# When the two attention branches' outputs are split into high and low halves: eleven scheduling ticks behind their loads instead of seven

## The chip, the cores and the metric

The kernel runs on one core of one Trainium2 chip, as one program with one launch. The metric is the device time of an execution in microseconds. The profile is one more execution, taken by the hardware profiler; its times count from the start of its span. The engines are TensorE (PE in the rows, with PEld for its weight loads), VectorE (DVE), ScalarE (ACT), GpSimd (POOL) and SyncE (SP). ACT, POOL and SP also issue DMAs; such an issue stands in the same in-order queue as the engine's other work.

## The reference, cut to what matters

One inference step of one decoder layer, for a prompt of 512 tokens (with 16 learned meta tokens ahead) and for a group of 8 sequences of 8 new tokens each with 2048 cached ones. Two attention branches run on the same normalised input; their outputs go through one output matrix each, are gated and added, and go through w_o:

```python
of = o_fox.reshape(n, l, FOX_WIDTH)
og = (ogn.reshape(n, l, GLA_V) * gla_norm_g.astype(F32) * jax.nn.silu(r.astype(F32))).astype(r.dtype)
branch_f = of @ w_fox_out
branch_g = og @ w_gla_out
merged = jax.nn.sigmoid(gate_f) * branch_f + jax.nn.sigmoid(gate_g) * branch_g
return merged @ w_o
```

Behind this stands a mixture of 32 experts, which the change does not touch. The stretch in question is the last part of the cached attention, which for the 8 sequences reads paged keys and values and computes

```python
s_past = jnp.einsum('nthd,nshd->nhts', q, k_past) * scale + a_q + r.transpose(0, 2, 1)[:, :, None, :]
p = jax.nn.softmax(jnp.concatenate([s_past, s_new], axis=-1), axis=-1).astype(v.dtype)
return jnp.einsum('nhts,nshd->nthd', p[..., :p_len], v_past) + jnp.einsum('nhts,nshd->nthd', p[..., p_len:], v)
```

## The kernel before, in words

Activations that feed large matrix products are kept as two numbers, a high half (hi, what a copy to a rounded 32-bit type leaves) and a low half (lo, the rest), so that three products at the faster rate stand for one exact product: `mm3` (line 138) issues hi*hi, hi*lo and lo*hi for each of the contraction's tiles. A split is two instructions: ACT copies the raw tile to the high half (line 123), and DVE or POOL subtracts (line 125).

Three strands of work are interleaved on TensorE in an order that the program writes out by hand (`manual_schedule` for PE): **dense**, the projections with w_in, of which the output gates are the last; **S**, the cached attention; and the other branch (GLA), which is finished when the stretch in question begins. One turn of the dense strand is half an output tile, 24 matmuls of 288 columns; for a gate ACT then applies a tanh (tile sm, line 1059) and issues the store of the result to DRAM (gtd, line 1060). In S a page of keys (K) or values (V) is one megabyte, gathered by an indirect DMA that POOL issues (line 892) as soon as TensorE has used the page that held one of the three buffers before. DVE transposes each K page (line 1017); TensorE makes scores (line 925); DVE, ACT and again DVE do the softmax (lines 939 to 962: biases R are added, the maximum goes through M, the exponentials are the tile SP, the diagonal block PN, and line 961 scales SP); TensorE transposes SP (line 968), multiplies with the V pages (line 988), ACT copies the result out (SO, line 998), and TensorE turns it round (line 1001).

The prompt's part of both branch outputs has been written to DRAM (ofd and ogd). `branch_inputs` brings it back: eight loads on the SP queue, of 128 rows by 512 (rawf, four) or 576 numbers (rawg, four), and then eight splits, high halves ofh and ogh on ACT, low halves ofl and ogl on POOL, two tiles at a time. The splits are pinned to the place in ACT's and POOL's order at which they are written. `branch_inputs` is a generator; each `yield` is a tick. The outer loop at line 1630 advances it once a turn (line 1631), between two steps of S and ahead of one turn of dense, so a number of ticks is a number of such turns. The splits' results are first needed by the merge (`merge`, from line 1092), which begins when S and dense are at an end; it reads two gate rows at a time from gtd (gt, line 1088). The merge's tiles take the room that rawf and rawg held.

Every DMA of SP or ACT signals its landing on one of eight semaphores (DMAHW0 to DMAHW7 in the order below), handed out in turn over both queues. A DMA that is given a semaphore waits, in its issuer's queue, until the one before it on that semaphore has landed, unless its issuer has already waited for that. Here the four rawf loads have numbers 0, 2, 3 and 4, the four rawg loads 5, 6, 7 and 1. The software DMAs of POOL have eight of their own (DMASW).

## Time and profile before

| what | value |
|---|---|
| device time, median of 3 runs | 975.14 us |
| lowest and highest of them | 973.74 and 982.65 us |
| profiled execution's own time | 978.69 us |
| its span | 976.7 us |
| TensorE busy | 889.1 us, 91% of the span |
| DVE, ACT, POOL busy | 54%, 29%, 29% |
| PE clock granted, mean | 0.959 |

The span is the stretch between the first and the last instruction that the profiler recorded; 2.0 us of the execution lie around it. The profiled execution took 3.55 us more than the median of the runs, which is inside their own spread of 8.91 us. Busy shares are means over stages that have different limits.

### The profile page before, as it was taken

Reading aid. Unit: us, or ns where it says so; the run is one execution under the profiler, and the core shown is the slowest. Engines: PE = TensorE matmul, PEld = TensorE weight load, DVE = VectorE, ACT = ScalarE, POOL = GpSimd, SP = SyncE. Lnnn points to the kernel's source line nnn. Section 1 sums busy time; section 2 is a strip of 40 time slices with the busy share of each in tenths; the row PEclk is TensorE's granted clock in tenths of the full one; section 3 lists DMA queues with packets and bytes.
Section 4 is the critical chain, followed back from the end, with each engine's and each line's share of the span. In section 5 each row is a group of like instructions: output and inputs, shape, how many; then the busy total and the mean of one; then the engine's idle time right before and its main releaser. Section 6 shows DMA issues by size and latency. Waiting matters only on the chain. (4 is left out here: it accounts for less than half of the span.)

```text
span 976.7 us, 18830 instructions
## 1 busy us (share of the span) xinstructions
PE 889.1 (91%) x7680; PEld 680.6 (70%) x7680; DVE 524.5 (54%) x1151; ACT 281.7 (29%) x615; POOL 279.1 (29%) x377
## 2 busy tenths in 40 slices
PE   3989989998799999897989898999499999999995
PEld 3878868788788899796888898999334434443343
DVE  5644545447766667663674256326436545564545
ACT  4114445342334324232233234116111111111113
POOL 5221101124244322241253144212573132211001
PEclk9999989998899999999799999999599999999999
DMA  7252222268369788789898756942679999999922
GB/s 212 66 130 62 90 79 65 60 240 310 117 216 344 285 276 280 224 315 375 287 341 304 253 177 189 310 183 97 225 275 407 410 406 413 409 410 412 385 91 99
DMA packets 124655, 239.98 MB, mean 246 GB/s; under 512 B 15812, under 2 KB 89452, under 8 KB 108180
## 3 DMA queue, kind: packets, MB, share of 16 engines
q1 hardware_dynamic: 107268, 160.78, 47.2%
q0 software_dynamic: 12432, 72.37, 20.0%
q10 hardware_dynamic: 4864, 5.57, 1.7%
q8 instruction: 62, 1.02, 0.4%
q14 instruction: 29, 0.24, 0.1%
HBM read 226.53 MB, written 15.83 MB: 248 GB/s over the span
## 5 line engine op out<-in xcount | busy, mean ns | idle before, releaser
L138 PE MATMUL pj<-hth,wh 128*128 128x288 f32 (+2 forms) x656 | 207.8, 317 | 2.1 <-DVE kt L381 1.8
L138 PE MATMUL pj<-hth,wl 128*128 128x288 f32 (+2 forms) x656 | 200.3, 305 | 0.4 <-DVE wl L125 0.4
L138 PE MATMUL pj<-htl,wh 128*128 128x288 f32 (+2 forms) x656 | 200.1, 305 | 0.0
L138 PEld LDWEIGHTS pj<-hth,wh 128*128 128x128 f32 (+1 forms) x656 | 127.1, 194 | 12.2 <-issue 7.5
L138 PEld LDWEIGHTS pj<-hth,wl 128*128 128x128 f32 (+1 forms) x656 | 126.5, 193 | 1.7 <-DVE wl L125 0.6
L138 PEld LDWEIGHTS pj<-htl,wh 128*128 128x128 f32 (+1 forms) x656 | 127.3, 194 | 0.5
L1353 PE MATMUL pj<-wgu,xt 128*64 128x512 f32 x512 | 117.7, 603 | 9.7 <-DVE xt L1363 9.7
L1326 POOL DMA_INDIRECT xg<-h2d,ix x64 | 65.8, 1028 | 122.9 <-DVE xt L1363 95.7
L1353 PEld LDWEIGHTS pj<-wgu,xt 128*64 128x64 f32 x512 | 36.0, 138 | 75.5 <-issue 65.6
L125 DVE TENSOR_TENSOR wl<-w,wh 128x1024 fp32r<-128x1024 f32 (+1 forms) x41 | 49.8, 1215 | 59.8 <-ACT wh L123 55.5
L1017 DVE STREAM_TRANSPOSE K<-K 128x2048 f32<-128x2048 f32 x32 | 73.5, 2302 | 4.0 <-DMA K<-in_cache_k_dram,idx 3.8
L123 ACT ACTIVATE wh<-w 128x1024 fp32r<-128x1024 f32 (+2 forms) x57 | 52.6, 925 | 59.4 <-PE pj L138 53.0
L1353 PE MATMUL ab<-yh,S 128*128 128x512 f32 (+1 forms) x160 | 66.8, 417 | 1.7 <-DVE x L1418 0.9
L1418 DVE TENSOR_TENSOR x<-x,ab 128x512 f32<-128x512 f32 (+1 forms) x80 | 54.5, 684 | 17.3 <-PE ab L1353 17.3
L1353 PE MATMUL ab<-yl,S 128*128 128x512 f32 (+1 forms) x160 | 63.2, 395 | 0.0
L1353 PE MATMUL dn<-wdn,heT 128*64 128x512 f32 x256 | 58.7, 593 | 1.4 <-ACT heT L1387 1.4
L892 POOL DMA_INDIRECT K<-in_cache_k_dram,idx x32 | 33.9, 1059 | 54.3 <-PE S L925 32.5
L1353 PEld LDWEIGHTS ab<-yh,S 128*128 128x128 f32 (+1 forms) x160 | 28.2, 176 | 27.3 <-DVE x L1418 15.0
L892 POOL DMA_INDIRECT V<-in_cache_v_dram,idx x32 | 32.5, 1016 | 49.0 <-PE tp L988 30.7
L1404 DVE SCALAR_TENSOR_TENSOR yl<-dn,gate,yh 128x512 fp32r<-128x512 f32 x32 | 24.0, 751 | 40.7 <-ACT yh L1403 38.1
L1353 PEld LDWEIGHTS dn<-wdn,heT 128*64 128x64 f32 x256 | 19.2, 137 | 37.8 <-issue 34.1
L1387 ACT ACTIVATE heT<-tp 128x256 f32<-128x256 f32 x16 | 6.1, 384 | 118.9 <-PE tp L1356 116.6
(428 smaller groups left out, 1604.4 us busy)
## 6 DMA issues: line engine op xcount, KB each, us to landing
wdn<-in_w_expert_down_dram SPq DMA_DIRECT2D x32, 1024.0 KB
wgu<-in_w_expert_gate_dram SPq DMA_DIRECT2D x32, 1024.0 KB
wgu<-in_w_expert_up_dram SPq DMA_DIRECT2D x32, 1024.0 KB
w<-in_w_in_dram SPq DMA_DIRECT2D x40, 512.0 KB
gtd<-sm ACTq DMA_DIRECT2D x32, 144.0 KB
gt<-gtd SPq DMA_DIRECT2D x8, 576.0 KB
R<-rdr SPq DMA_DIRECT2D x16, 256.0 KB
w<-in_w_o_dram SPq DMA_DIRECT2D x8, 512.0 KB
```

Of the source, the lines that this page charges most:

```text
L123: keep(nc.scalar.activation(hi, raw, AF.Copy))
L125: keep(e.tensor_tensor(lo, raw, hi.bitcast(F32), op=OP.subtract))
L138: nc.tensor.matmul(ps, lhsT=w[:, kt, :], rhs=r[:, kt, cs], start=(kt == 0 and j == 0), stop=(kt == nk - 1 and j == 2))
L892: nc.gpsimd.indirect_dma_start(t, None, view, bass.IndirectOffsetOnAxis(ap=self.idx[:, which, i:i + 1], axis=0)))
L1017: self.tc.keep_in_program_order(nc.vector.transpose(t, t))
L1326: self.nc.gpsimd.indirect_dma_start(xg[:, b * 256:(b + 1) * 256], None, self.h2d.rearrange("t (q f) -> (t q) f", q=4), bass.IndirectOffset ...
L1353: self.tc.keep_in_program_order(self.nc.tensor.matmul(*a, **kw))
L1387: self.nc.scalar.activation(hT, pt[:, 0:256], AF.Copy)
L1404: nc.vector.scalar_tensor_tensor(yl[:, nh], dn, gate, yh[:, nh].bitcast(F32), op0=OP.mult, op1=OP.subtract)
L1418: self.tc.keep_in_program_order(nc.vector.tensor_tensor(x, x, ps[:w], op=OP.add))
```

## The change

The number of ticks between the issue of the loads and the first split goes from 7 to 11.

```diff
--- before.py
+++ after.py
@@ -1075,7 +1075,7 @@
                 raws.append((raw, n))
                 for m in range(4):
                     nc.sync.dma_start(raw[:, m], src[m, :, 0:n])
-            for _ in range(7):
+            for _ in range(11):
                 yield
             for (raw, n), (h, l) in zip(raws, hl):
                 for m in range(4):
```

TensorE's order is the same, row for row, in both programs. On ACT the first two high halves move from between the setting of a query block (QB) and a gate's tanh to a place some 45 rows later. In these rows a name carries its buffer's number, and what stands in brackets are the semaphores that the instruction waits for. ACT before, at the first two splits:

```order
L901 ACTIVATE QB1_1889<-QT_1884 32x16x8 x3
L123 ACTIVATE ofh_5312<-rawf_5311 128x512 [waits DMAHW0_49,Pool_49]
L123 ACTIVATE ofh_5312<-rawf_5311 128x512 [waits DMAHW2_49]
L1059 ACTIVATE sm_3282<-pj_5325 128x288 [waits DMAHW5_49,PE_49]
L1060 DMA gtd_75<-sm_3282 128x288 [waits Activation_49]
L998 ACTIVATE SO_5391<-tp_5087 128x128 [waits PE_49]
L953 ACTIVATE SP_5277,sl_5276<-R_4821,sb_5274 128x512 [waits DVE_49]
L955 ACTIVATE PN_1890,sl_5276<-sN_5261,sb_5274 128x8 [waits Pool_49]
L953 ACTIVATE SP_5277,sl_5276<-R_4821,sb_5274 128x512
L955 ACTIVATE PN_1890,sl_5276<-sN_5261,sb_5274 128x8
L1059 ACTIVATE sm_3282<-pj_5395 128x288 [waits DMAHW1_49,PE_49]
L1060 DMA gtd_75<-sm_3282 128x288 [waits DMAHW5_49,Activation_49]
```

ACT at the same place now:

```order
L901 ACTIVATE QB1_1889<-QT_1884 32x16x8 x3
L1059 ACTIVATE sm_3282<-pj_5325 128x288 [waits DMAHW5_49,PE_49]
L1060 DMA gtd_75<-sm_3282 128x288 [waits DMAHW0_49,Activation_49]
L998 ACTIVATE SO_5391<-tp_5087 128x128 [waits PE_49]
L953 ACTIVATE SP_5277,sl_5276<-R_4821,sb_5274 128x512 [waits DVE_49]
L955 ACTIVATE PN_1890,sl_5276<-sN_5261,sb_5274 128x8 [waits Pool_49]
L953 ACTIVATE SP_5277,sl_5276<-R_4821,sb_5274 128x512
L955 ACTIVATE PN_1890,sl_5276<-sN_5261,sb_5274 128x8
L1059 ACTIVATE sm_3282<-pj_5395 128x288 [waits DMAHW1_49,PE_49]
L1060 DMA gtd_75<-sm_3282 128x288 [waits DMAHW5_49,Activation_49]
L961 ACTIVATE SP_5277<-SP_5277,srl_5291 128x512 [waits DVE_49]
```

The two ofh are gone from here, and the two gtd issues stay; the first of them has gained a wait for DMAHW0, which the first ofh had done before it, and the second waits for DMAHW5 in both programs.

POOL before, from its first low halves on (K and V are page gathers):

```order
L125 TENSOR_TENSOR ofl_5313<-rawf_5311,ofh_5312 128x512 [waits DMAHW0_49,Activation_49]
L125 TENSOR_TENSOR ofl_5313<-rawf_5311,ofh_5312 128x512 [waits DMAHW2_49,Activation_49]
L892 DMA K_5850<-in_cache_k_dram,idx_383 128x2048 [waits DMASW3_49,DVE_49,PE_49]
L125 TENSOR_TENSOR ofl_5313<-rawf_5311,ofh_5312 128x512 [waits DMAHW3_49,Activation_49]
L928 MEMSET PN_1890 128x256 [waits DVE_49,PE_49,Pool_49]
L125 TENSOR_TENSOR ofl_5313<-rawf_5311,ofh_5312 128x512 [waits DMAHW4_49,Activation_49]
L125 TENSOR_TENSOR ogl_5320<-rawg_5318,ogh_5319 128x576 [waits DMAHW5_49,Activation_49]
L125 TENSOR_TENSOR ogl_5320<-rawg_5318,ogh_5319 128x576 [waits DMAHW6_49,Activation_49]
L892 DMA V_5975<-in_cache_v_dram,idx_383 128x2048 [waits DMASW7_49,DMASW4_49,PE_49]
L125 TENSOR_TENSOR ogl_5320<-rawg_5318,ogh_5319 128x576 [waits DMAHW7_49,Activation_49]
L125 TENSOR_TENSOR ogl_5320<-rawg_5318,ogh_5319 128x576 [waits DMAHW1_49,Activation_49]
L892 DMA V_6047<-in_cache_v_dram,idx_383 128x2048 [waits DMASW1_49,PE_49]
```

POOL now, from the last clearing of PN on:

```order
L928 MEMSET PN_1890 128x256 [waits DVE_49,PE_49,Pool_49]
L892 DMA V_5963<-in_cache_v_dram,idx_383 128x2048 [waits DMASW7_49,DMASW4_49,PE_49]
L892 DMA V_6031<-in_cache_v_dram,idx_383 128x2048 [waits DMASW1_49,PE_49]
L125 TENSOR_TENSOR ofl_5313<-rawf_5311,ofh_5312 128x512 [waits DMAHW0_49,Activation_49]
L125 TENSOR_TENSOR ofl_5313<-rawf_5311,ofh_5312 128x512 [waits DMAHW2_49,Activation_49]
L892 DMA V_6153<-in_cache_v_dram,idx_383 128x2048 [waits DMASW6_49,DMASW2_49,PE_49]
L892 DMA V_6212<-in_cache_v_dram,idx_383 128x2048 [waits DMASW4_49,PE_49]
L125 TENSOR_TENSOR ofl_5313<-rawf_5311,ofh_5312 128x512 [waits DMAHW3_49,Activation_49]
L125 TENSOR_TENSOR ofl_5313<-rawf_5311,ofh_5312 128x512 [waits DMAHW4_49,Activation_49]
L125 TENSOR_TENSOR ogl_5320<-rawg_5318,ogh_5319 128x576 [waits DMAHW5_49,Activation_49]
L125 TENSOR_TENSOR ogl_5320<-rawg_5318,ogh_5319 128x576 [waits DMAHW6_49,Activation_49]
L892 DMA V_6287<-in_cache_v_dram,idx_383 128x2048 [waits DMASW5_49,DMASW0_49,PE_49]
```

Before, three more V gathers follow with no split between them; now two ogl follow. The same five V gathers stand in other places between the low halves: two ahead of all eight, two behind the first pair, and the last behind six.

ACT before, from the gate's tanh ahead of the last sequence's softmax on (SO is the result of the sequence before):

```order
L1059 ACTIVATE sm_3282<-pj_6122 128x288 [waits DMAHW2_49,PE_49]
L953 ACTIVATE SP_6102,sl_6101<-R_5748,sb_6099 128x512 [waits DVE_49]
L955 ACTIVATE PN_1890,sl_6101<-sN_6086,sb_6099 128x8 [waits Pool_49]
L953 ACTIVATE SP_6102,sl_6101<-R_5748,sb_6099 128x512
L955 ACTIVATE PN_1890,sl_6101<-sN_6086,sb_6099 128x8
L1060 DMA gtd_75<-sm_3282 128x288 [waits Activation_49]
L998 ACTIVATE SO_6184<-tp_5950 128x128 [waits PE_49]
L961 ACTIVATE SP_6102<-SP_6102,srl_6116 128x512 [waits DVE_49,Activation_49]
L961 ACTIVATE SP_6102<-SP_6102,srl_6116 128x512 [waits Activation_49]
L1059 ACTIVATE sm_3282<-pj_6188 128x288 [waits DMAHW3_49,PE_49]
L1060 DMA gtd_75<-sm_3282 128x288 [waits Activation_49]
L123 ACTIVATE wh_6215<-w8_5994 128x1024 [waits DMAHW6_49]
```

ACT now, from the same tanh on:

```order
L1059 ACTIVATE sm_3282<-pj_6106 128x288 [waits DMAHW2_49,PE_49]
L953 ACTIVATE SP_6086,sl_6085<-R_5748,sb_6083 128x512 [waits DVE_49]
L955 ACTIVATE PN_1890,sl_6085<-sN_6070,sb_6083 128x8 [waits Pool_49]
L953 ACTIVATE SP_6086,sl_6085<-R_5748,sb_6083 128x512
L955 ACTIVATE PN_1890,sl_6085<-sN_6070,sb_6083 128x8
L1060 DMA gtd_75<-sm_3282 128x288 [waits DMAHW5_49,Activation_49]
L123 ACTIVATE ofh_5312<-rawf_5311 128x512 x2
L961 ACTIVATE SP_6086<-SP_6086,srl_6100 128x512 [waits DVE_49,Activation_49]
L961 ACTIVATE SP_6086<-SP_6086,srl_6100 128x512 [waits Activation_49]
L998 ACTIVATE SO_6171<-tp_5942 128x128 [waits PE_49]
L1059 ACTIVATE sm_3282<-pj_6175 128x288 [waits DMAHW3_49,PE_49]
L1060 DMA gtd_75<-sm_3282 128x288 [waits DMAHW6_49,Activation_49]
```

The first two ofh stand ahead of the scaling of SP, and SO has moved behind that scaling. The next two ofh follow the last row shown, and four ogh come behind the next two gate halves.

On SP the eight loads keep their place. The first two gate-row loads (gt) go from ahead of the second branch weight to behind the third, the second of them waits for the last ogl, and one expert weight (wdn) that stood ahead of the load of x2 stands three branch weights later.

## Rows read from the trace of the kernel before

**Rows 1.** Who TensorE (PE) waited for, 440 to 560 us: us in total, times, longest.

```profile
PE tp L1001 <- ACT SO L998: 6.7, 1, 6.7
...
PE tp L968 <- ACT SP L961: 1.8, 1, 1.8
...
PE pj L138 <- DVE wl L125: 0.4, 1, 0.4
```

**Rows 2.** Timeline of ACT and its DMA issues (ACTq), around the first splits.

```profile
459.06 0.63 ACT L123 ACTIVATE ofh<-rawf 128x512 fp32r<-128x512 f32 x1 [7.89 <-DMA rawf<-ofd]
462.16 0.63 ACT L123 ACTIVATE ofh<-rawf 128x512 fp32r<-128x512 f32 x1 [2.48 <-DMA rawf<-ofd]
...
463.12 0.33 ACTq L1060 DMA_DIRECT2D gtd<-sm  x1
463.49 0.28 ACT L998 ACTIVATE SO<-tp 128x128 f32<-128x128 f32 x1 [0.40 <-ACT sm L1059]
...
466.07 0.33 ACTq L1060 DMA_DIRECT2D gtd<-sm  x1
467.16 1.34 ACT L961 ACTIVATE SP<-SP,srl 128x512 f32<-128x512 f32 x2 [1.12 <-DVE srl L959]
```

**Rows 3.** Timeline of TensorE: three instructions that end a wait or follow ACT.

```profile
463.82 0.48 PE L1001 MATMUL tp<-ident,SO 128*128 128x128 f32 x1 [6.74 <-ACT SO L998]
...
526.44 0.27 PE L1001 MATMUL tp<-ident,SO 128*128 128x128 f32 x1
...
541.86 1.64 PE L988 MATMUL tp<-V,PT 128*32 128x128 f32 x32 [3.18 <-DMA V<-in_cache_v_dram,idx]
```

**Rows 4.** Line 138's matmuls in two stretches: busy (count), PE clock, DMA share, GB/s.

```profile
468.00:474.00 6.00, 5.30 (x22) 0.50 0.97 314
476.10:479.10 3.00, 3.00 (x23) 1.00 0.69 155
```

**Rows 5.** Timeline of POOL: low halves, and the last V page's issue.

```profile
495.27 2.53 POOL L125 TENSOR_TENSOR ofl<-rawf,ofh 128x512 fp32r<-128x512 f32 x2
...
509.65 2.81 POOL L125 TENSOR_TENSOR ogl<-rawg,ogh 128x576 fp32r<-128x576 f32 x2
...
532.99 0.95 POOL L892 DMA_INDIRECT V<-in_cache_v_dram,idx  x1 [7.39 <-PE tp L988]
```

**Rows 6.** One stretch: length; PE, PEld, DVE, ACT, POOL; PE clock; DMA; GB/s.

```profile
530.00:540.00 10.00, 8.14 (x139) 7.07 (x138) 0.92 (x3) 1.88 (x3) 1.63 (x2) 1.00 1.02 408
```

**Rows 7.** Timeline of the SP queue: two groups of issues.

```profile
457.48 1.75 SPq L1077 DMA_DIRECT2D rawg<-ogd  x4
...
518.92 2.57 SPq L1088 DMA_DIRECT2D gt<-gtd  x2
```

**Rows 8.** Who the SP queue's DMA issues waited for, 461 to 467 us.

```profile
SPq L130 <- DMA rawf<-ofd: 2.9, 1, 2.9
SPq L908 <- DMA rawf<-ofd: 1.8, 1, 1.8
```

**Rows 9.** Timeline of DVE: short operations, and the merge's first.

```profile
467.35 0.36 DVE L962 TENSOR_SCALAR PN<-PN,srl 128x8 f32<-128x8 f32 x2
...
494.87 3.10 DVE L962 TENSOR_SCALAR PN<-PN,srl 128x8 f32<-128x8 f32 x2
...
520.16 0.96 DVE L945 TENSOR_TENSOR M<-M,aq 128x2 f32<-128x2 f32 x1
...
555.88 0.42 DVE L1102 SCALAR_TENSOR_TENSOR mt<-gt,pj 128x256 f32<-128x256 f32 x1 [5.81 <-PE pj L138]
```

**Rows 10.** Timeline of ACT around the last sequence's softmax.

```profile
508.72 1.26 ACT L123 ACTIVATE ogh<-rawg 128x576 fp32r<-128x576 f32 x2 [0.40 <-ACT sm L1059]
...
524.41 0.28 ACT L998 ACTIVATE SO<-tp 128x128 f32<-128x128 f32 x1
525.84 1.33 ACT L961 ACTIVATE SP<-SP,srl 128x512 f32<-128x512 f32 x2 [1.15 <-DVE ogc L880]
...
531.50 0.41 ACT L1059 ACTIVATE sm<-pj 128x288 f32<-128x288 f32 x1 [2.56 <-PE pj L138]
```

## The prediction

> **What bounds the kernel now.** The stretch in which the change acts ends when TensorE has done the last step of the cached attention, so I read first who TensorE waited for between 440 and 560 us [rows 1]. The longest wait is 6.7 us for SO, ACT's copy of a finished result; 1.8 us for SP, the scaled softmax, follow, both on ACT. ACT's timeline shows why [rows 2]: the first ofh begins at 459.06, having waited 7.89 us for its load, the second at 462.16, when the second load has landed, and behind them stand a gate's tanh, its store, and SO (463.49). TensorE goes on at 463.82 [rows 3]. [...]
>
> What ends the stretch is another thing: TensorE's last step with a V page begins at 541.86 after 3.18 us of waiting for that page [rows 3], which POOL had issued at 532.99 [rows 5]; the DMA engines were full then, at 408 GB/s [rows 6]. From there TensorE runs on into the merge. So a gain at 460 counts as far as it also brings that page forward.
>
> **Part 1, the first two splits leave the gap.** They free ACT of their own two waits, but not of the loads. The store of the gate that stood behind them (gtd) shares its landing semaphore, DMAHW0, with the first rawf load. Before, ofh had waited for that; now the store must, and ACT's queue with it. The load landed by 459.06. From the store to SO ACT took 463.49 - 463.12 = 0.37 us [rows 2], so SO comes at 459.43 and TensorE goes on 0.33 us later, at 459.76: 4.06 us sooner than 463.82.
>
> Then the same again. Next on ACT is the second store, at 466.07 before [rows 2], which waits for DMAHW5, the first rawg load, in both programs. Before, it was reached late and did not show. Now it is reached near 462, and the scaling of SP (467.16) stands behind it. When that load lands no row says, but both sides are bounded. It had landed by 466.07, since the store then went out. It was issued at 457.48 [rows 7], behind four rawf loads, of which one held up an SP issue for 1.8 us [rows 8]. SP's issues before it had waited for the first two loads, and the second landed at 462.16 [rows 2]; so the third landed no sooner than 462.16 + 1.8 = 464.0. The scaling thus begins between 464.0 + 0.37 = 464.4 and 466.07 + 0.37 = 466.4, against 467.16: 0.7 to 2.8 us sooner. It can also be nothing, since the next K page is now asked for 4 us earlier and shares the DMA engines. I take **-0.8 us**, near the late end, because the fourth rawf load stands ahead of the rawg one and the second landed 3.1 us after the first [rows 2], the third 1.8 or more behind that. Of the 6.7 us gap most is not removed: it comes back as a longer wait for SP.
>
> That a DMA issue holds its queue for another load's landing is seen on SP, which waited 2.9 us with a weight load for rawf, whose data it does not need [rows 8]; no row shows ACT doing so. [...]
>
> **Part 2, the first two low halves leave POOL.** At 495.27 they ran for 2.53 us [rows 5], and a DVE pair that takes 0.36 us took 3.10 us beside them [rows 9]. It delayed a weight's low half, for which TensorE waited 0.4 us [rows 1]: **-0.4 us**. Likewise a tiny DVE operation took 0.96 us at 520.16 beside an ogl pair that now moves away; its 0.8 us come off the last sequence's softmax and pay for part of the next item.
>
> **Part 3, what the splits meet where they now stand.** On ACT the first pair, 2 * 0.63 us [rows 2], runs while DVE sums, so the scaling at 525.84 is not held up by it. But SO, at 524.41 before [rows 10], now follows the scaling: 525.84 + 1.33 = 527.17, less the 0.8 and the 1.2 us of parts 1 and 2, is 525.2; plus 0.33 it meets TensorE at 525.5, where TensorE would have been at 526.44 - 1.2 = 525.2 [rows 3]. I take **+0.2 us**; without the 0.8 it is 1.0.
>
> On POOL the last V page now stands behind two ofl and two ogl. The ogl pair hangs on the tanh that began at 531.50 [rows 10]. That tanh moves by -0.8 - 0.4 + 0.2 = -1.0 us to 530.5; then 0.41 for it, 0.40 until ogh begins, 0.63 for one ogh [rows 10] and 2.81 for the pair [rows 5]: the page is issued at 534.75, **1.8 us later** than at 532.99. If its landing takes as long as before (541.86 - 532.99 = 8.87 us), the stretch ends 1.8 us later. Against that, two gate-row loads of 576 KB (2 * 128 * 576 numbers), issued at 518.92 before [rows 7], now come after this page. They were in front of it on engines that were full: 1.18 MB at 408 GB/s are 2.9 us [rows 6]. The end lies between +1.8 - 2.9 = -1.1 and +1.8; I take the middle, **+0.4 us**. It replaces the gains above and is not added to them, since TensorE waits for the page either way. Two earlier V pages go behind the first ofl pair; their steps come ahead of this page's, and the wait moves rather than grows.
>
> **Part 4, edits that cost nothing.** The last two ogl run beside the last dense turns. The two gate-row loads wait for them, near 544; the merge first uses one at 555.88, where DVE waited for TensorE [rows 9], so 12 us cover some 3 us of transfer; without that cover the merge's first product would wait the 3 us. The expert weight that goes three branch weights later is needed only in the experts' stage. TensorE's order does not change.
>
> **Sum.** Against the profiled execution: 978.69 + 0.4 = 979.1 us, whose span was 976.7. That execution was 3.55 us above the median of the runs, so the forecast for the median is 975.14 + 0.4 = **975.5 us**: no change. About 1% (9.75 us) is what a measurement of this kernel can tell from no change; its own three runs spread over 8.91 us.
>
> **Rivals.** *The whole gap goes*: the stores do not hold ACT, or their loads land early in most executions. TensorE gains 6.7 + 1.8 + 2.4 us, and the last page moves along with the tanh: against the forecast's -0.8 this is 10.1 us better, 965.4. For it speaks that the wait shown is for the splits; against it, that the stores' semaphores are in the program. Chance 0.05. *Part of it goes*: the rawg load lands at the early end (-2.8 against -0.8, so -2.0) and the full clock comes back sooner (up to -2.4): 971.1 to 973.5. Chance 0.12.
>
> *The low halves now collide with the softmax* and the kernel is slower. Two operations of DVE that read SBUF alone were stretched by POOL's subtractions [rows 9]; now an ofl pair of 2.53 us [rows 5] falls on the last sequence's chain of sums, reciprocal and scaling on DVE. It decides from the point where one of them, between the sum and the reciprocal, begins behind the first ofl; then the chain, SO and the last page come 2.5 us later. With the page's old 8.87 us this gives 1.8 + 2.5 = +4.3 us, 979.4, and 980.4 if part 1 gains nothing. For it: the pair starts within a microsecond of that chain. Against it: the adding starts as soon as ACT's sums are there, one ofh (0.63 us) ahead of the first ofl. Chance 0.22.
>
> [...]
>
> **How the numbers follow.** Forecast (974 to 978): 0.58; the whole gap 0.05; part of it 0.12; the collision 0.22; slower by over 1%, with both losses and a merge that waits, 0.03. The range from 971 to 980.5 takes in the bounds -1.1 and +1.8, the partial gain and the collision, and leaves out the first and the last. Faster by over 1%: 0.05; within 1%: 0.92; slower: 0.03.
>
> **What would show it.** TensorE's wait for SO falls to about 2.7 us, and its wait for SP grows from 1.8 to about 5; the store ahead of SO begins near 459, the second near 466. The DVE pair near 495 takes 0.36 us again. SO of the last sequence stands behind the scaling. POOL's last V issue follows an ogl pair directly, near 535, and TensorE still waits for that page. I am wrong if either store goes out before its load has landed, if the SP wait does not grow, or if the last page's step moves by more than 3 us.

## The result, and the profile after

The change makes the kernel slower: 980.29 us is the median of 20 runs, against 975.58 us of 20 runs of the kernel before, a ratio of 1.0059 with a 95% interval of 1.0039 to 1.0078. The same kernel compared once more, on another occasion, gave 1.0035 (0.9999 to 1.0070). The profiled execution took 982.93 us, its span is 981.0. The time lies at the upper edge of the range given (971 to 980.5), but the forecast was no change, 975.5, and the change costs some 0.35 to 0.6%.

Up to the store of ogd (line 683) both programs run alike, so I count from it. In the kernel before it is this row of the SP queue,

```profile
442.20 0.36 SPq L683 DMA_DIRECT2D ogd<-og  x1
```

and the scores of the last sequence, a second mark, begin here on TensorE:

```profile
516.03 1.06 PE L925 MATMUL S<-K,QB 128*32 128x128 f32 x32
```

In the changed kernel the SP queue shows the same store, and the two gate-row loads that have moved behind the third branch weight:

```profile
442.69 0.36 SPq L683 DMA_DIRECT2D ogd<-og  x1
...
544.46 2.52 SPq L1088 DMA_DIRECT2D gt<-gtd  x2
```

Who TensorE waited for, in the changed kernel, 440 to 560 us (us in total, times, longest):

```profile
PE tp L968 <- ACT SP L961: 10.3, 1, 10.3
PE tp L988 <- DMA V<-in_cache_v_dram,idx: 4.0, 1, 4.0
PE tp L1001 <- ACT SO L998: 2.0, 2, 1.6
```

Against [rows 1] the wait for SO has nearly gone (of the 2.0 us only 0.4 are at this place), and the wait for SP has grown from 1.8 to 10.3 us: the two waits were 8.5 us together, and are 10.7 at this place now. The second profile of the changed kernel (change_again below) splits them otherwise, 4.1 and 4.3 us, 8.4 together:

```profile
PE tp L1001 <- ACT SO L998: 5.7, 2, 4.1
...
PE tp L968 <- ACT SP L961: 4.3, 1, 4.3
```

ACT's timeline in the first profile says why the wait for SP grew:

```profile
457.26 0.33 ACTq L1060 DMA_DIRECT2D gtd<-sm  x1
457.63 0.28 ACT L998 ACTIVATE SO<-tp 128x128 f32<-128x128 f32 x1 [4.85 <-PE pj L138]
...
459.93 0.39 ACT L1059 ACTIVATE sm<-pj 128x288 f32<-128x288 f32 x1
468.45 0.33 ACTq L1060 DMA_DIRECT2D gtd<-sm  x1
468.82 1.33 ACT L961 ACTIVATE SP<-SP,srl 128x512 f32<-128x512 f32 x2 [8.51 <-DMA rawg<-ogd]
```

The first store goes out at 457.26 and SO follows it, 6 us sooner than in [rows 2]. The gate's tanh runs at 459.93, and then ACT's queue stands still for 8.1 us until the second store goes out at 468.45. The scaling follows, later than before. The hold is named as the landing of rawg.

POOL's timeline has the K page, which k_waits below shows to be behind the late landing, and the later places of the pairs:

```profile
459.61 0.94 POOL L892 DMA_INDIRECT K<-in_cache_k_dram,idx  x1 [3.76 <-PE S L925]
...
525.25 2.51 POOL L125 TENSOR_TENSOR ofl<-rawf,ofh 128x512 fp32r<-128x512 f32 x2 [6.73 <-ACT ofh L123]
527.91 0.96 POOL L892 DMA_INDIRECT V<-in_cache_v_dram,idx  x1
529.18 0.94 POOL L892 DMA_INDIRECT V<-in_cache_v_dram,idx  x1 [0.30 <-PE tp L1001]
...
536.95 2.80 POOL L125 TENSOR_TENSOR ogl<-rawg,ogh 128x576 fp32r<-128x576 f32 x2 [2.46 <-ACT ogh L123]
539.90 0.96 POOL L892 DMA_INDIRECT V<-in_cache_v_dram,idx  x1 [0.16 <-issue]
```

Since SO was early, the next K page was asked for at 459.61; before, it was asked for at 466.47, after the rawg load had landed. In the second profile the first store was itself held for rawf, until 18.25 us behind the store of ogd (14.57 in the first profile), so that SO and the K page came later there, the page 21.59 us behind that store against 16.92.

Further down, two V pages stand behind the first ofl pair, and the last one, at 539.90, behind the first ogl pair ([rows 5]: 532.99). What the two late pages cost is seen on the DMA engines. From 7 to 13 us behind the scores of the last sequence they were full before, and nearly empty with the change (columns as in [rows 6]; the kernel before first, then the changed one):

```profile
523.03:529.03 6.00, 5.84 (x50) 5.34 (x43) 3.48 (x15) 4.33 (x12) 1.80 (x2) 1.00 1.01 328
524.09:530.09 6.00, 4.12 (x30) 3.67 (x29) 3.97 (x13) 4.17 (x11) 4.38 (x4) 0.97 0.17 27
```

The second profiles of the two kernels show the same, with DMA shares of 1.02 and 0.18. Not all of this is the two pages: the change also takes the two gate-row loads out of this stretch, and one V page, which is issued 0.5 us behind the scores instead of 5.2. low_later_11 below has these changes as well, but not the two late pages, and moves 228 GB/s in the same stretch.

DVE's timeline, a short pair and two small operations of the last softmax:

```profile
495.07 0.36 DVE L962 TENSOR_SCALAR PN<-PN,srl 128x8 f32<-128x8 f32 x2
...
521.22 0.16 DVE L945 TENSOR_TENSOR M<-M,aq 128x2 f32<-128x2 f32 x1
...
525.37 1.21 DVE L880 COPY ogc<-ogb 128x32 f32<-128x32 f32 x1
```

The pair of [rows 9] takes 0.36 us again instead of 3.10, and the operation at line 945 0.16 instead of 0.96. But the copy at line 880 takes 1.21 us; it starts 0.12 us after POOL's ofl pair at 525.25.

TensorE at the last sequence's scores, at the turn of SO, and at the last V page's step:

```profile
517.09 1.06 PE L925 MATMUL S<-K,QB 128*32 128x128 f32 x32
...
528.67 0.33 PE L1001 MATMUL tp<-ident,SO 128*128 128x128 f32 x1 [1.60 <-ACT SO L998]
...
545.83 0.86 PE L988 MATMUL tp<-V,PT 128*32 128x128 f32 x24 [4.01 <-DMA V<-in_cache_v_dram,idx]
```

It waits 1.60 us for SO, which now follows the scaling, and then works at a granted clock of 0.50 for a while. The clock is the third figure from the end in this window (length; PE, PEld, DVE, ACT, POOL busy; PE clock; DMA share; GB/s):

```profile
530.80:533.00 2.20, 2.20 (x11) 2.20 (x11) 2.16 (x2) 0.62 (x2) 2.02 (x2) 0.50 0.94 385
```

The chain that ended last passes through the load of rawg, the copy, the ogl pair and the last page's transfer (start, us, what):

```profile
456.58 11.79 DMA rawg<-ogd
...
525.37 1.22 DVE ogc L880
...
536.95 0.58 POOL ogl L125
...
539.90 5.89 DMA V<-in_cache_v_dram,idx
```

Set out by marks, with the second profile of each kernel beside it (each figure is the difference of two start times):

| stretch, us | before | changed | before, 2nd | changed, 2nd | forecast |
|---|---|---|---|---|---|
| store of ogd to the scaling at the first place | 24.96 | 26.13 | 24.73 | 24.82 | -0.8 |
| store of ogd to the scores of the last sequence | 73.83 | 74.40 | 71.36 | 71.37 | -1.2 |
| scores to the scaling of SP | 9.81 | 10.03 | 10.05 | 10.03 | -0.8 |
| scaling to TensorE's turn of SO | 0.60 | 1.55 | 0.33 | 1.55 | +1.0 |
| turn of SO to the next tanh | 5.06 | 6.70 | 5.17 | 5.13 | 0 |
| that tanh to the last V page's issue | 1.49 | 4.53 | 1.50 | 4.53 | +2.8 |
| issue to TensorE's step with the page | 8.87 | 5.93 | 8.09 | 7.25 | -2.9 to 0 |
| scores to that step, sum of five | 25.83 | 28.74 | 25.14 | 28.49 | |

From the step with the last V page to the end of the span it is 434.8 and 439.4 us before, 435.2 and 434.9 after: nothing is lost there. The loss lies in 3.1 us between the scores and the last step, (28.74 + 28.49 - 25.83 - 25.14) / 2, and in what the first place adds: 0.6 us in the first pair of profiles (74.40 - 73.83), nothing in the second (71.37 and 71.36).

### The profile page after: what moved, and what is told of

It is laid out like the page before. It is cut to its first block, busy times and chain, and to the rows that moved or that the text cites. A ratio compares the mean times of both kernels' runs of the same rounds, so it can differ in the third digit from the quotient of the medians.

```text
span 981.0 us, 18832 instructions
## 1 busy us (share of the span) xinstructions
PE 892.2 (91%) x7680; PEld 684.8 (70%) x7680; DVE 521.8 (53%) x1151; ACT 281.8 (29%) x615; POOL 279.3 (28%) x377
## 3 DMA queue, kind: packets, MB, share of 16 engines
q8 instruction: 62, 1.02, 0.4%
## 4 chain that ended last, share of the span: by engine, by line
PE 70%; DVE 9%; DMA 9%; ACT 5%; issue 3%; POOL 3%; ACTq 0%; POOLq 0%; DVEq 0%; SPq 0%
PE pj L138 25%; PE pj L1353 12%; PE ab L1353 6%; PE dn L1353 6%; PE pj L1140 5%; PE S L925 2%; PE tp L988 2%; DMA V<-in_cache_v_dram,idx 1%; DMA out_dram<-s 1%; DMA rawg<-ogd 1%; PE G L523 1%; DVE K L1017 1%; DMA gtd<-sm 1%; PE tp L736 1%; DMA K<-in_cache_k_dram,idx 1%
```

## The experiments

Eighteen runs follow: fifteen other kernels, one of them twice, and both kernels of the change once more. Theory A puts the loss at the last sequence (A1 in its softmax, A2 in the last V page's place on POOL, L both), theory B at the first place or in how pages happen to land, D in the DMA engines, K in the K page asked for early. All figures of this table are worked out from one profile each as in the table above: the scaling at the first place and the scores of the last sequence are counted from the store of ogd, the rest from those scores; "copy" is the duration of line 880 in the last softmax. An interval stands behind each ratio.

| kernel | first scaling | scores | copy | two V pages | tanh | last V issue | its step | ratio to before |
|---|---|---|---|---|---|---|---|---|
| before | 24.96 | 73.83 | 0.18 | 6.90, 8.62 | 15.47 | 16.96 | 25.83 | |
| before_again | 24.73 | 71.36 | 0.42 | 6.87, 8.56 | 15.55 | 17.05 | 25.14 | |
| the change | 26.13 | 74.40 | 1.21 | 10.82, 12.09 | 18.28 | 22.81 | 28.74 | 1.0059 (1.0039 to 1.0078) |
| change_again | 24.82 | 71.37 | 1.20 | 10.84, 12.10 | 16.71 | 21.24 | 28.49 | 1.0035 (0.9999 to 1.0070) |
| low_later_11 | 24.76 | 71.21 | 0.18 | 6.81, 8.53 | 16.86 | 18.35 | 25.53 | 0.9972 (0.9937 to 1.0008) |
| low_later_again | 26.31 | 73.96 | 0.18 | 6.81, 8.47 | 16.80 | 18.29 | 25.57 | 1.0024 (0.9991 to 1.0057) |
| ticks_12 | 26.23 | 76.35 | 0.18 | 6.81, 8.54 | 15.65 | 20.13 | 26.26 | 1.0076 (1.0037 to 1.0115) |
| ticks_14 | 26.29 | 75.11 | 0.18 | 6.84, 8.55 | 15.68 | 17.17 | 25.54 | 1.0070 (1.0039 to 1.0101) |
| first_low_later_11 | 26.63 | 73.74 | 1.30 | 6.02, 7.27 | 18.37 | 22.90 | 28.90 | 1.0053 (1.0031 to 1.0074) |
| g_low_later_11 | 25.51 | 71.75 | 1.20 | 10.83, 12.10 | 16.69 | 18.18 | 27.44 | 1.0037 (1.0014 to 1.0059) |
| first_pair_12 | 26.20 | 74.50 | 0.18 | 6.81, 8.51 | 15.65 | 21.85 | 27.73 | 1.0016 (0.9984 to 1.0049) |
| two_loads_11 | 16.20 | 71.38 | 1.20 | 11.19, 12.46 | 17.05 | 21.58 | 30.22 | 1.0023 (0.9991 to 1.0055) |
| two_loads_low_later_11 | 19.75 | 65.26 | 1.30 | 6.02, 7.27 | 16.79 | 18.28 | 25.39 | 1.0015 (0.9988 to 1.0041) |
| two_loads_first_pair_12 | 16.17 | 72.08 | 0.18 | 6.79, 8.48 | 15.63 | 21.84 | 28.27 | 1.0016 (0.9989 to 1.0043) |
| quarter_loads_11 | 17.32 | 64.50 | 1.20 | 11.20, 12.46 | 17.05 | 21.58 | 27.81 | 0.9946 (0.9912 to 0.9980) |
| last_pair_11 | 24.21 | 71.34 | 1.40 | 11.54, 12.80 | 17.25 | 18.75 | 28.45 | 1.0039 (1.0008 to 1.0070) |
| last_pair_13 | 23.57 | 70.73 | 0.18 | 6.82, 8.51 | 15.66 | 20.20 | 29.20 | 1.0069 (1.0033 to 1.0105) |
| pairs_11_13 | 23.37 | 72.97 | 1.40 | 11.51, 12.77 | 18.79 | 23.34 | 31.82 | 1.0085 (1.0053 to 1.0117) |
| k_waits | 24.27 | 71.42 | 1.20 | 10.84, 12.11 | 16.69 | 21.22 | 28.60 | 1.0028 (0.9996 to 1.0060) |
| low_later_k_waits | 23.90 | 70.84 | 2.53 | 6.03, 7.28 | 19.08 | 20.58 | 27.48 | 1.0001 (0.9973 to 1.0029) |

**Low halves later: low_later_11 and low_later_again.** The low halves of a pair are written one tick behind its high halves:

```diff
-                    self.split(raw[:, m], h[:, m, 0:n], l[:, m, 0:n], "pool", pin=True)
+                    keep(nc.scalar.activation(h[:, m, 0:n], raw[:, m], AF.Copy))
+                    late.append((raw[:, m], h[:, m, 0:n], l[:, m, 0:n]))
                     if m % 2:
                         yield
+                        for r, x, y in late:
+                            keep(nc.gpsimd.tensor_tensor(y, r, x.bitcast(F32), op=OP.subtract))
+                        late = []
```

> Eleven ticks as in the change, but each pair of low halves on POOL is written one tick behind its high halves, so that no low half stands inside the last sequence's softmax and two V pages pass ahead of the first. ACT's order stays that of the change. Theory A (the time is lost at the last sequence: POOL's low halves stretch a DVE copy from 0.18 to 1.21 us, TensorE waits 1.6 us for SO and its clock falls, and the last V page stands behind a pair of ogl): the copy takes 0.2 us again, TensorE waits about 0.6 us for SO, the last V page is issued when TensorE releases its buffer, about 3 us sooner; 3 to 4.5 us faster than the change, 0.996 to 1.001 of the kernel before. Theory B (the time is lost at the first place, where a store waits 8.5 us for a rawg load, and what follows only carries it): as the change, 1.004 to 1.008.

> The kernel with all low halves one tick behind their high halves, a second time and on this chip. Theory L: 25.4 to 25.6 us from the scores of the last sequence to the step with the last V page, 0.994 to 1.001. Theory B: 1.0035 to 1.006, as the change.

Both profiles give the forecast local figure, 25.5 us from scores to step, 3 us less than the change. DVE's timeline in the first of them shows the copy free, and the ofl pair falling on the pair of line 962 instead, which nothing waits for:

```profile
526.06 0.18 DVE L880 COPY ogc<-ogb 128x32 f32<-128x32 f32 x1
...
526.79 2.81 DVE L962 TENSOR_SCALAR PN<-PN,srl 128x8 f32<-128x8 f32 x2
```

The ratios, 0.9972 and 1.0024, lie on either side of 1, the second of them outside the ranges of both theories; taken together the kernel is as fast as before. That speaks for the last sequence. SO still follows the scaling here, and the tanh still comes 1.3 us later than before (16.86 and 16.80 us behind the scores), but the three V pages are not held up behind low halves. Late pages cost the time, then, more than the late tanh by itself.

**Other tick counts: ticks_12 and ticks_14.** The number 11 becomes 12 or 14.

> Twelve ticks. Neither high nor low halves stand inside the last sequence's softmax, and SO stands ahead of the scaling of SP again, as before the change; four ofl stand ahead of the last V page, the second pair hanging on a later tanh. Theory A: no wait of TensorE for SO and full clock there, 3 us sooner than the change at the tanh ahead of the last V page; that page is still issued some 4 us behind this tanh; 0.999 to 1.002 of the kernel before. If it were the POOL queue alone, with nothing from softmax and clock: as the change, 1.004 to 1.008. Theory B: as the change too.

> Fourteen ticks. All five V pages are issued ahead of every low half, and the softmax is free of splits. Theory A: all that the change lost at the last sequence comes back, the last V page is issued about 6 us sooner than in the change, and TensorE no longer waits 4 us for it; 0.992 to 0.998 of the kernel before, unless the merge then waits for the last low halves, which would show as TensorE's wait for POOL near 550. Theory B: 1.004 to 1.008.

The local figures came (25.5 us for fourteen, as before the change), but both runs are slower, by 0.7%. With later splits the gate-row loads stand ahead of other loads on SP, and the second of them waits there for the last ogl. SP's queue in ticks_12 is held for 13 us, and a branch weight goes out behind it:

```profile
552.72 13.05 SPq L1088 DMA_DIRECT2D gt<-gtd  x2
...
573.63 0.46 SPq L130 DMA_DIRECT2D w<-in_w_gla_out_dram  x1
```

TensorE's waits in the merge of ticks_12 (in the change there is no such row):

```profile
PE pj L138 <- ACT wh L123: 4.3, 1, 4.3
```

The prediction had priced an uncovered merge at 3 us, for its gate rows; what TensorE waits for here is a branch weight's high half, whose load stood behind those rows on SP. The gain at the last sequence is bought with 4.3 us of waiting, and 4.9 in ticks_14. With these waits taken off, 1.0032 and 1.0020 would be left: theory A is not met for fourteen ticks (0.992 to 0.998), and where the rest is from was not tried.

**Two DMAs for eight: two_loads_11.**

```diff
-                for m in range(4):
-                    nc.sync.dma_start(raw[:, m], src[m, :, 0:n])
+                nc.sync.dma_start(raw, src[:, :, 0:n].rearrange("m p n -> p m n"))
```

> Eleven ticks, but the four rawf loads are one DMA and the four rawg loads one, so that they take two of the eight landing semaphores and neither of the next two stores of a gate shares one with them. Theory A and B agree that the second store then goes out at once and that TensorE's wait of 10.3 us for SP shrinks by some 8 us, with the full clock kept or back sooner. Theory A: what is lost at the last sequence stays, so the run is 8 to 10 us faster than the change, 0.995 to 0.998 of the kernel before. Theory B: all that was lost goes, 0.985 to 0.992. If a store's shared semaphore is not what holds ACT, the wait for SP stays at about 10 us and the ratio at 1.004 to 1.008.

ACT's timeline shows the second store going out at once, and the scaling 16.20 us behind the store of ogd, 9.9 and 8.6 us earlier than in the change's two profiles:

```profile
460.58 0.39 ACTq L1060 DMA_DIRECT2D gtd<-sm  x1
461.39 1.34 ACT L961 ACTIVATE SP<-SP,srl 128x512 f32<-128x512 f32 x2 [0.85 <-DVE srl L959]
```

So the shared semaphore is what held ACT. But of those 8.6 to 9.9 us little is left at the scores of the last sequence, 71.38 against 74.40 and 71.37. TensorE now waits for pages instead, among other things 4.7 us for a K page, by way of DVE's transposition of it:

```profile
PE tp L988 <- DMA V<-in_cache_v_dram,idx: 6.7, 1, 6.7
PE S L925 <- DVE K L1017: 4.7, 1, 4.7
```

The DMA engines are full all the while (one stretch, columns as in [rows 6]):

```profile
460.00:500.00 40.00, 31.61 (x466) 28.78 (x464) 22.60 (x48) 10.01 (x23) 8.31 (x10) 0.89 1.03 376
```

The forecast of 8 to 10 us was wrong by the same mistake that "the whole gap goes" would have made: the gap at 460 is not free to be won. The gap was 10 us wide, yet pages set the pace behind it.

**Change_again, and one half of the cure each: first_low_later_11 and g_low_later_11.** Here the wait of one tick ahead of the low halves is kept for the first pair alone, or for the two rawg pairs alone:

```diff
                     if m % 2:
-                        yield
+                        if n == 512 and m == 1:
+                            yield
                         for r, x, y in late:
```

with n != 512 as the condition in g_low_later_11; the other pairs have their tick behind the low halves.

> The changed kernel itself, a second profile and a second comparison, as the measure for the three beside it. Ratio to the kernel before 1.004 to 1.008. Counted from the store of ogd by line 683, TensorE's step with the last V page began at 99.7 us before and at 103.1 with the change; if the loss is of this stretch, it begins at 101.5 or later again, and a DVE copy (line 880) of the last softmax takes 1.2 us again.

> As the change, but the first pair of ofl is written one tick later, so that POOL does not subtract beside the last softmax; the last V page still stands behind the first ogl pair. Theory A1 (the loss is in the softmax, from the copy that POOL stretches by 1.0 us and the half clock after TensorE's gap, up to 1.6 us): 1 to 2.6 us faster than the change on this chip, the last V page still issued 4.5 us behind the tanh that precedes it. Theory A2 (the loss is the page's place behind the ogl pair): as the change, within 0.5 us.

> As the change, but the ogl pairs are written one tick later, so that the last V page passes ahead of all four; the ofl pair beside the softmax stays. Theory A2: the page is issued 1.5 us behind the tanh that precedes it instead of 4.5, and the run is 3 us faster than the change. Theory A1: the page is issued sooner, but takes longer to land, since the DMA engines are full, and its step moves by less than 1 us; as the change, with the copy of line 880 at 1.2 us.

In change_again the copy took 1.20 us as expected, and the ratio of 1.0035 lies just below the range given. The step with the last V page missed its bound: it came 99.86 us behind the store of ogd, not at 101.5 or later. That bound had been taken from single profiles; the second profile of the kernel before has 96.50, so that the two pairs of profiles differ by 3.5 and 3.4 us at this step.

first_low_later_11 did not do what it was made for: both V pages went out sooner than ACT's high halves were ready, and POOL's pair still began beside the softmax. Its DVE timeline:

```profile
526.65 1.30 DVE L880 COPY ogc<-ogb 128x32 f32<-128x32 f32 x1
```

It tells only that two V pages issued 5 us earlier bring nothing while the last one stays late. In g_low_later_11 the last V page was free; POOL's timeline shows the two other pages still late, behind the ofl pair,

```profile
520.77 0.96 POOL L892 DMA_INDIRECT V<-in_cache_v_dram,idx  x1 [0.16 <-issue]
522.04 0.95 POOL L892 DMA_INDIRECT V<-in_cache_v_dram,idx  x1 [0.30 <-PE tp L1001]
...
528.12 0.95 POOL L892 DMA_INDIRECT V<-in_cache_v_dram,idx  x1 [0.69 <-PE tp L988]
```

and TensorE's step with the last page came 9.3 us after its issue:

```profile
537.38 0.87 PE L988 MATMUL tp<-V,PT 128*32 128x128 f32 x12 [4.30 <-DMA V<-in_cache_v_dram,idx]
```

27.44 us after the scores is 1.2 less than the mean of the change's two profiles, not 3: A2 alone is refuted. Against the 25.5 us of low_later_11, where the tanh and the last V page came at the same times (16.86 and 18.35 us; here 16.69 and 18.18), it is 1.9 more, and up to that page the two kernels differ at the last sequence in the ofl pairs' places alone, and by them in the two late pages. As with the change, the DMA engines stood nearly empty from 7 to 13 us behind the scores, at 26 GB/s; low_later_11 moved 228. Behind that gap three pages follow one another (405 GB/s from 16 to 19 us), and the last of them lands late though it was issued in time. So the two losses overlap and do not add up: by single profiles the two late pages alone cost 1.9 us here, the last page issued at 22.90 us alone costs 3.4 in first_low_later_11 (28.90 against 25.5), and the change has both for 3.1.

**The two together: two_loads_low_later_11.** Both diffs above.

> One DMA for rawf and one for rawg, and all low halves one tick later than in the change. With four loads each, low halves a tick later gave 0.9972 of the kernel before, and two loads alone gave 1.0023. If both gains hold side by side (the second store no longer waits for rawg, the softmax and the last page are free of POOL): 0.990 to 0.996. If the DMA engines, full in this stretch, set when the pages land whatever ACT does: as low halves later alone, 0.995 to 1.000.

1.0015, above both ranges given: neither gain shows beside the kernel before. The profiled execution was the shortest of its twelve, at 966.34 us, so its early scores (65.26) are not typical.

**Out of the softmax: first_pair_12, and with two loads two_loads_first_pair_12.** The first two pairs are split together at the twelfth tick.

```diff
-            for _ in range(11):
+            for _ in range(12):
...
-                    if m % 2:
+                    if m % 2 and (n != 512 or m == 3):
                         yield
```

> The kernel before, for a second profile. Counted from the store of ogd by line 683, ACT's scaling of SP behind the second store of a gate began at 25.0 us in the first profile, and in seven profiles with eleven ticks or more and eight loads at 24.8 to 26.6. If the change lost time at this place, it begins at 25.5 or earlier again; if the place is neutral, anywhere in 24.8 to 26.6. From the scores of the last sequence (line 925) to the tanh that precedes the last V page: 15.5 us again.

> As the change, but the first pair is split one tick later, with its high halves, together with the second pair; the two rawg pairs and all that follows on SP stay as in the change. ACT has no split in the last softmax, and SO stands ahead of the scaling of SP again. Theory A1 (the loss is in the last softmax): the copy of line 880 takes 0.18 us, from the scores of the last sequence to the tanh ahead of the last V page it takes 15.6 us instead of the 16.7 and 18.3 of the change's two profiles, and the run is 1.1 to 2.7 us faster than the change, 1.001 to 1.004 of the kernel before. Theory B (the loss is at the first place, or in how the pages land): as the change, 1.0035 to 1.006.

> Two whole loads, and the first pair split one tick later together with the second. If what the change lost is the last softmax and what two loads gain at the first place is kept: 0.998 to 1.001. If the DMA engines take the gain of the first place back in full: 1.000 to 1.003.

The softmax is free and the tanh comes after 15.65 us, as A1 said: 1.1 us earlier than in change_again, 2.6 earlier than in the change's first profile, where the granted clock had fallen to 0.50. But four ofl instead of two now stand ahead of the ogl pair and the last V page, the page is issued 6.2 us behind that tanh instead of 4.5, and the step comes at 27.73. The ratio of 1.0016 lies in theory A1's range, but its interval reaches into theory B's. With two loads as well the ratio is again 1.0016, in the range for engines that take the gain of the first place back, and again with an interval (0.9989 to 1.0043) that covers both answers. The second profile of the kernel before has its scaling at 24.73 us, as expected if the change loses at the first place; but the change's own second profile has 24.82, so this tells little. It has the same waits as [rows 1] (TensorE, 440 to 560 us):

```profile
PE tp L1001 <- ACT SO L998: 6.5, 1, 6.5
...
PE tp L968 <- ACT SP L961: 1.9, 2, 1.8
```

**Less to load: quarter_loads_11.**

```diff
-                for m in range(4):
-                    nc.sync.dma_start(raw[:, m], src[m, :, 0:n])
+                nc.sync.dma_start(raw[:, 0], src[0, :, 0:n])
...
-                    self.split(raw[:, m], h[:, m, 0:n], l[:, m, 0:n], "pool", pin=True)
+                    self.split(raw[:, 0], h[:, m, 0:n], l[:, m, 0:n], "pool", pin=True)
```

> One load of a quarter of rawf and one of a quarter of rawg; all four splits of a branch read that quarter, so three quarters of the branch outputs are left out. 1.6 MB less is read than with two whole loads, which gave 1.0023. Theory D (the DMA engines, full here, set when pages land, and so the end of the stretch): up to 1.6 MB / 408 GB/s = 3.9 us sooner than two whole loads, 0.998 to 0.999. Theory A1 and A2: as two whole loads, 1.001 to 1.003, since softmax and POOL's order are those of the change.

This kernel leaves out three quarters of the branch outputs. 0.9946 against 1.0023 with two whole loads: 0.77%, some 7.5 us, for 1.67 MB less, with ACT's and POOL's splits in the same places (the two were timed on different occasions, and their intervals span 0.6% each). This speaks for theory D, and the size is above the 3.9 us worked out (4.1 us for 1.67 MB at 408 GB/s); where the rest is from was not tried.

**The other way round: last_pair_11, last_pair_13, pairs_11_13.** In the kernel before, which splits from the seventh tick on, only the last pair is moved to one of the change's places, or the two rawg pairs to both:

```diff
                     if m % 2:
-                        yield
+                        for _ in range({(NQ, 1): 2}.get((n, m), 1)):
+                            yield
```

This is last_pair_11; in last_pair_13 the table is (NQ, 1): 4, in pairs_11_13 it is (512, 3): 3 and (NQ, 1): 2.

> The kernel before, but its last pair (two ogh, two ogl) is split where the change splits its first: beside the last softmax and ahead of two V pages. The last V page stays free. Theory L (the last sequence): the copy of line 880 takes 1.2 us, the two pages are issued 10.8 and 12.1 us behind the scores of the last sequence instead of 6.9 and 8.6, and TensorE's step with the last V page begins 27.4 to 27.9 us behind these scores, as in the kernel with only the ogl pairs later, instead of 25.1 to 25.8: 1.001 to 1.004. Theory B (the first place, or how the pages happen to land): 25.1 to 25.8 us, 0.998 to 1.001.

> The kernel before, but its last pair is split at the thirteenth tick, ahead of the last V page alone; the softmax and the other V pages are free. Theory L: the last V page is issued 4.5 us behind the tanh that precedes it instead of 1.5, lands some 6 us later instead of 8.9, and its step begins 26 to 26.5 us behind the scores: 1.000 to 1.002. Theory B: 25.1 to 25.8 us, 0.998 to 1.001.

> The kernel before, with the first ogl pair at the eleventh tick and the second at the thirteenth: both places of the change, and the first place as before. Theory L: the step with the last V page begins 28 to 29 us behind the scores of the last sequence, as with the change, and the run is as slow as the change: 1.002 to 1.006. Theory B: 0.998 to 1.001.

All three are slower than the kernel before, with the first scaling no later than it was (24.21, 23.57 and 23.37 us). One pair beside the softmax costs 28.45 - 25.5 = 3 us, one ahead of the last V page 29.20 - 25.5 = 3.7, both 31.82 - 25.5 = 6.3 (25.5 is the mean of 25.83 and 25.14), so L holds, and the local cost is above the forecast in all three, the ratio in last_pair_13 and pairs_11_13. In last_pair_13 the page is issued where L said,

```profile
533.25 2.81 POOL L125 TENSOR_TENSOR ogl<-rawg,ogh 128x576 fp32r<-128x576 f32 x2 [7.78 <-ACT ogh L123]
536.21 0.96 POOL L892 DMA_INDIRECT V<-in_cache_v_dram,idx  x1 [0.15 <-issue]
```

but TensorE waits 7.09 us for it, and its step comes 9.0 us after the issue, not 6:

```profile
545.21 1.93 PE L988 MATMUL tp<-V,PT 128*32 128x128 f32 x32 [7.09 <-DMA V<-in_cache_v_dram,idx]
```

The gate-row loads went out ahead of the page here, on SP:

```profile
531.55 4.90 SPq L1089 DMA_DIRECT2D gt<-gtd  x2
```

In ticks_12, with the page issued as long after the scores (20.13 us) and the gate-row loads behind it, the step came 6.1 us after the issue. The difference is 2.9 us, the term that the prediction had worked out as 1.18 MB at 408 GB/s.

**The K page held: k_waits, and with the cure low_later_k_waits.**

```diff
+            scr = rp.tile([128, 2], F32, name="scr")
+            for t in range(11):
+                if t == 2:
+                    g = raws[1][0][:, 0, 0:2]
+                    self.tc.keep_in_program_order(nc.gpsimd.tensor_tensor(scr, g, g, op=OP.subtract))
                 yield
```

> The change, with one tiny POOL operation (a subtraction of two numbers a row, its result unused) ahead of the K page of the first place; it reads the first rawg tile and so holds this page until that load has landed. Theory K (the K page that is asked for 7 us earlier delays the rawg load by about its transfer, 1 MB at 408 GB/s = 2.6 us, and with it the second store and the scaling of SP): the page is asked for at 23 to 24 us behind the store of ogd instead of 17 to 18, and the scaling begins at 23.2 to 24.5 instead of 25.9 on the mean; the last sequence loses what it lost. 0 to 1.5 us faster than the change, since the K page itself now lands later: 1.001 to 1.006. If the load lands late whatever the page does: the scaling stays at 24.8 to 26.6 and the page comes only later, 1.005 to 1.009.

> The same hold of the K page together with all low halves one tick later. Both theories: from the scores of the last sequence to the step with the last V page 25.4 to 25.6 us. Theory K: the scaling of SP at the first place begins at 23.2 to 24.5 us, and the run is at the kernel before or a little faster, 0.996 to 1.001. Otherwise 1.000 to 1.004.

POOL's timeline in k_waits shows the page behind the tiny operation,

```profile
465.61 0.19 POOL L1082 TENSOR_TENSOR scr<-rawg 128x2 f32<-128x2 f32 x1 [10.90 <-DMA rawg<-ogd]
466.36 0.97 POOL L892 DMA_INDIRECT K<-in_cache_k_dram,idx  x1 [0.56 <-issue]
```

and ACT's the second store and the scaling with it:

```profile
465.46 0.33 ACTq L1060 DMA_DIRECT2D gtd<-sm  x1
465.83 1.33 ACT L961 ACTIVATE SP<-SP,srl 128x512 f32<-128x512 f32 x2 [5.36 <-DMA rawg<-ogd]
```

The scaling begins at 24.27 and 23.90 us behind the store of ogd, in the range that theory K gave, against 24.76 to 26.63 (mean 25.9) in the nine profiles with eight loads, late splits and a free K page. Holding back a transfer brought ACT forward.

It matters how soon behind the rawg loads the page is asked for, a grouping that I made only after the runs. In eight of the profiles with eight loads the page is asked for 3.0 to 3.3 us behind the first rawg issue, and the second store goes out 11.1 us behind that issue on the mean (10.25 to 11.87). In the six others in which rawg holds the store, with the page asked for 4.7 to 9.6 us behind, it is 8.7 us (8.66 to 8.86). The 2.4 us between are near the page's transfer, 2.6 us. The first profile of the change is in the first group (3.0 and 11.9 us), its second profile in the other (5.8 and 8.7), and so are last_pair_13 and pairs_11_13, which ask for the page 5 us sooner than the kernel before (18.99 and 19.03 us) without loss at the scaling. So the change lost here in one of its two profiles, and not in the other.

The cure of the last sequence did not work in low_later_k_waits: the ofl pair fell on the copy again, for 2.53 us, and the local figure was 27.48 instead of 25.5. The ratio of 1.0001 is that of the kernel before all the same. No version that computes the whole result beats the kernel before.

## Why the prediction was wrong, point by point

**What bounds the stretch** was right: the last V page ends it, and a gap at 460 counts only as far as pages come earlier. two_loads_11 shows this in full. The 2.4 us that the first two rivals count for the clock are read from [rows 4]: 22 * (5.30/22 - 3.00/23). In the first profile of the change they were not won: 19 matmuls of line 138 took 4.70 us from 470.37 on, at a granted clock of 0.50 again.

**Part 1** was right in mechanism, but its gain did not come. ACT is held by the second store until rawg has landed, for 8.5 us in the first profile of the changed kernel and 3.5 in the second, and two DMAs in place of eight take the hold away (in two_loads_11 the scaling begins 16.20 us behind the store of ogd, against 26.13 and 24.82). But the scaling was forecast 0.8 us earlier, and came 1.2 us later in the first pair of profiles, 0.1 in the second. The prediction had seen that the next K page is asked for earlier and shares the engines, and had priced that at no more than the loss of the gain. It can be worse: asked for 3 us behind the rawg loads, the page delays the store by 2.4 us, near its own transfer of some 2.6 us (1 MB at 408 GB/s). k_waits shows it, and the change's second profile, where the page came later, shows the other case. On the mean of nine profiles with eight loads and late splits the first scaling begins at 25.9 us, on that of five with the splits from the seventh tick at 24.2; the scores of the last sequence begin at 73.6 and 72.05, some 1.5 us apart. The single profiles spread over 5.1 and 3.1 us, so this term is a mean that does not stand clear of its spread.

**Part 2** was right for both of its pieces (0.36 and 0.16 us again, and no wait for a weight's low half), but the 0.8 us at line 945 were eaten by the copy, which took 1.21 us beside POOL's ofl pair instead of 0.18.

**Part 3** holds the two steps that failed most. The first is a term put at nothing. The two earlier V pages behind the first ofl pair got no price ("the wait moves rather than grows"), beside a sum that counts on full DMA engines. With these pages asked for some 4 us later, the engines stood nearly empty for 6 us instead (27 GB/s against 228 in low_later_11), and the wait grew: the step with the last page came 1.9 us later in g_low_later_11 than in low_later_11, and 3.0 later in last_pair_11 than in the kernel before.

The second is the tanh ahead of the last V page, behind which that page is issued. It was put 1.0 us earlier, and came 3.4 later behind the store of ogd in the first pair of profiles and 1.2 in the second. From the scores on it is 2.8 and 1.2 us. Of this the scaling of SP gains nothing where 0.8 was forecast; SO, now behind the scaling, costs 1.0 and 1.2 us at TensorE, the worse end that the text named ("without the 0.8 it is 1.0"); and in the first profile TensorE then ran at a granted clock of 0.50 for two microseconds, another 1.6 us that the prediction did not have for this place (from the turn of SO to the tanh it took 6.7 us there, in first_low_later_11 and in pairs_11_13, and 5.1 in change_again). The POOL term was right: 4.53 us behind the tanh against the 4.25 of the working. So was the pay-back: the page landed 0.8 and 2.9 us sooner after its issue.

**Part 4** was right: the merge did not wait for gate rows or weights, at eleven ticks. At twelve and fourteen it does, for 4.3 and 4.9 us.

**The collision rival** had the time (979.4 to 980.4) and the place, but its price was 1.0 us, not 2.5: the copy took 1.21 us instead of 0.18. That the time was met is luck: a copy stretched by 1.0 us does not make the 3.1 us of the last sequence. (By its own terms its upper end is 979.4 + 0.8 = 980.2, not 980.4.) The copy took 0.18 us in the clear (0.42 in the second profile of the kernel before), 1.2 to 1.4 us in ten profiles and 2.53 in one, as if mostly it waited for one subtraction (2.51 us for two), once for the pair. By what means POOL's subtractions hold it no run shows.

**The sum.** The forecast for the end of the stretch was +0.4 us; it came 3.5 and 3.4 us later in the two pairs of profiles, of which 3.1 are of the last sequence on the mean. With the 1.5 at the first place, from the means over more kernels, they are 4.6; measured were 4.7 (medians) and, by the ratios, 5.8 and 3.4. The first term is shown by kernels that put it in and take it out; the second rests on means over single profiles and on k_waits, whose ratio (1.0028) does not stand apart from the change's.

## What to carry to other kernels

Before a wait is moved off an engine, look for what else in that engine's queue waits for the same landing; and when something is freed early, ask which transfer it asks for, and which load that will be put ahead of. Where DMA engines are full, an issue that leaves early gains less than it seems (in two_loads_11, at 376 GB/s, the scaling came 8.6 to 9.9 us earlier than with the change and the scores of the last sequence 0.0 to 3.0), and one that leaves late can leave them empty for a time that does not come back (in g_low_later_11 6 us at 26 GB/s, and the last step 1.9 us later than in low_later_11): count from the last transfer backwards, and look at what the engines move while an issue waits. A scheduling number like a tick count moves whole groups across unrelated neighbours, so each value is a new program with its own collisions (11 lost at the last sequence, 12 and 14 mostly in the merge).

## What the runs showed of the hardware that I had not expected

- TensorE's granted clock fell to 0.50 after a wait of 1.6 us for SO in the changed kernel, for about 2 us, and from there to the tanh it took 6.70 us; in change_again, after the same wait, it took 5.13.
- A plain DVE copy of 128 by 32 numbers, 0.18 us in the clear, took 1.2 to 1.4 us when it began beside POOL's subtractions, and 2.53 us once.
- Marks of two executions of one program differ by 2.5 and 3.0 us at the scores of the last sequence (71.36 and 73.83 before, 71.37 and 74.40 after), with the same instructions up to there: single profiles of this stretch cannot be compared below that.
